# Block sums for a Winograd-Strassen down projection: made by DMAs that add in DRAM, with signs moved into the tokens' sums and three subtractions

## The chip, the cores and the metric

One core of a Trainium2 chip runs the kernel. The metric is the device time of one execution in microseconds: the median of three runs, and beside it the time of the one execution that the profiler recorded. TensorE (PE) multiplies; PEld is its loading of weights; VectorE (DVE), ScalarE (ACT) and GpSimd (POOL) work element by element; SyncE (SP) issues most of the DMAs. Each engine has its own stream of instructions and takes them in order: an instruction that waits holds back all that stand behind it on that engine, DMA issues too.

## What is computed

One block of an encoder on 512 tokens of width 1024, all in float32: three token mixers (an mLSTM, a neighbourhood attention, a cross-attention into a memory), merged by gates, then a gated feed-forward part and a last norm.

```python
def reference(x, mem, mix_norm_g, w_in, ...):
    for l in range(DEPTH):                      # DEPTH = 1
        h = rms_norm(x, mix_norm_g[l])
        proj = h @ w_in[l]
        ml_q, ml_k, ml_v, ml_o, ml_gates, na_qkv, xa_q, merge_pre = jnp.split(proj, split_points, axis=-1)
        ...
        merged = g_ml * (y_ml @ w_br_ml[l]) + g_na * (y_na @ w_br_na[l]) + g_xa * (y_xa @ w_br_xa[l])
        x = x + merged @ w_out[l]
        x = x + conv_glu_ffn(rms_norm(x, ffn_norm_g[l]), w_ffn_up[l], w_ffn_conv[l], b_ffn_conv[l], w_ffn_down[l])
    return rms_norm(x, final_norm_g)

def conv_glu_ffn(h, w_up, w_conv, b_conv, w_down):
    a, u = jnp.split(h @ w_up, 2, axis=-1)
    return (jax.nn.gelu(dwconv3(a, w_conv, b_conv)) * u) @ w_down
```

The change touches the last matrix product, `@ w_down`: 512 x 2816 times 2816 x 1024.

## The kernel before

**Precision.** A float32 product is made of three matmuls in a fast float32 format: every operand is split into a high part (ACT rounds a copy, `wh`) and a low part (DVE subtracts, `wl`), and `mm3` (L191) issues high x high, high x low and low x high.

**Weights.** All weights but those of the down projection lie in `wflat` in the order of their use, in blocks of 128 x 1024 (1088 in two of them): mlq, mlk, then eight token-major blocks ("tm"; two of 1088 columns, four and two of 1024), xaq, o, memk, memv, naq, nak, the gates and branches, out, and for the up projection pairs ua, uu. `weights(key)` (L180) hands out a block; before that it issues, by `emit_raw`, the loads up to three blocks ahead on SP's queue (tile `wr`, three buffers), and the splits up to one block ahead (`emit_split`). A load waits until the block three places before it has been split.

**Stages.** mlq and mlk (keys and queries), tm (values: `nv` tiles are written by ACT and DVE at L502 and L504 into scratch buffers and stored to `nav_d` by POOL at L506), the attention parts, the branches, the output projection, then 22 pairs of ua and uu (the loop at L1354), then the down projection.

**The down projection** is Strassen's scheme in Winograd's form on 2 x 2 blocks: the weights w_down are four blocks B11, B12, B22, B21 of 11 tiles of 128 x 512 each (`wdn` in DRAM), the hidden units four quarters `a11`, `a21`, `a12`, `a22`. Instead of eight block products it makes seven, p1 to p7, in the order of `ORDER`. Three of them need nothing but a block; the others need the sums T1 to T4 of blocks. Before the change these are made in SBUF, in the loop of the up projection, one of 11 tiles at a time: `sum_load` (L1250) has POOL load the tile of all four blocks; DVE makes T1 and T3 in one subtraction (L1272), T2 and T4 in one each (L1260, L1269); T3 and T2 are split (L1261 on ACT, L1264 on DVE); POOL stores high and low parts of T3 and T2 to `tsp` (L1266) and T1 and T4 unsplit to `tdn` (L1270). The loop takes three of these steps in a turn (L1389). In the down projection `raws_to` and `tiles_to` load them again.

**Order.** The program is written in the order of the text, but a scheduler places the instructions of each engine: an instruction that its own estimate calls ready may be placed ahead of others that stand before it in the text.

Of the kernel before, what the change touches and what calls it, by code (L numbers as in the profile page):

```python
# [11 lines left out]
F32 = mybir.dt.float32  # L12
# [5 lines left out]
P = 128  # L18
# [83 lines left out]
def hybrid_block(ctx, tc, xg, xT, memT, wflat, wdn, vecs, gbias, nabias, out):  # L102
# [18 lines left out]
    def unit(dt=F32):  # L121
        return up.tile([P, UNIT], dt, tag="unit", name=nm("u"))
# [11 lines left out]
        return atp.tile([P, 512], F32, tag="at", name=nm("at"))  # L134


    raws, split = {}, {}
    RAW_AHEAD, SPLIT_AHEAD = 3, 1
    st = {"raw": 0, "split": 0}
# [18 lines left out]
    def emit_split(i):  # L158
# [4 lines left out]
        for a, b in hs:  # L163
# [12 lines left out]
            for k in range(a, b):  # L176
                q = slice((k - a) * c, (k - a + 1) * c)
                split[i].append((h[:, q], l[:, q]))

    def weights(key):  # L180

        i, _, n = BINDEX[key]
        while st["raw"] <= min(i + RAW_AHEAD, len(BLOCKS) - 1):
            emit_raw(st["raw"])
            st["raw"] += 1
        while st["split"] <= min(i + SPLIT_AHEAD, len(BLOCKS) - 1):
            emit_split(st["split"])
            st["split"] += 1
        return split.pop(i)

    def mm3(ps, lh, ll, rh, rl, start, stop):  # L191
        PE.matmul(ps, lh, rh, start=start, stop=False)  # L192
# [885 lines left out]


    gens = []  # L1080

    quota = [0.0]

# [155 lines left out]
        A.activation(xt[t][:, hf * S:(hf + 1) * S], pt, AF.Copy)  # L1239


    HS = S // 2
    B11, B12, B22, B21 = range(4)
    T1, T4 = range(2)
    T3, T2 = range(2)
    tdn = dp.tile([2, P, HF * S], F32, name="tdn")
    tsp = dp.tile([2, 2, P, HF * S], F32R, name="tsp")
    sums = []

    def sum_load(k):  # L1250
        w = unit()[:, :4 * S]
        w4 = w.rearrange("p (q n) -> p q n", q=4)
        ks = slice(k * S, (k + 1) * S)
        G.dma_start(w4, wdn[:, :, ks].rearrange("q p n -> p q n"))
        q = [w[:, i * S:(i + 1) * S] for i in range(4)]
        hl = []

        def high():
            hl.append(unit(F32R)[:, :4 * S].rearrange("p (x q n) -> p x q n", x=2, q=2))
            V.tensor_tensor(q[B22], q[B22], q[B11], op=ALU.subtract)  # L1260
            A.activation(hl[0][:, 0], w4[:, 1:3], AF.Copy)  # L1261

        def low():
            V.tensor_tensor(hl[0][:, 1], w4[:, 1:3], hl[0][:, 0].bitcast(F32), op=ALU.subtract)  # L1264
            for x in range(2):
                G.dma_start(tsp[:, x, :, ks].rearrange("q p n -> p q n"), hl[0][:, x])  # L1266

        def store():
            V.tensor_tensor(q[B21], q[B21], q[B22], op=ALU.subtract)  # L1269
            G.dma_start(tdn[:, :, ks].rearrange("q p n -> p q n"), w4[:, 0:4:3])  # L1270

        sums.extend([lambda: V.tensor_tensor(w[:, :2 * S], w[:, S:3 * S], w[:, :2 * S], op=ALU.subtract), high, store, low])  # L1272


    PRODUCTS = {"p1": (wdn, B11), "p5": (tdn, T1), "p6": (tsp, T2), "p3": (wdn, B22), "p7": (tsp, T3), "p2": (wdn, B21),
                "p4": (tdn, T4)}
    GROUPS = ((0, 4), (4, 8), (8, HF))
# [51 lines left out]
    def early(g, i):  # L1329
        a11, a21, a12, a22 = quarters(g)  # L1330
        if i == 0:
            V.tensor_tensor(a21, a21, a22, op=ALU.add)
        else:
            V.tensor_tensor(a11, a21, a11, op=ALU.subtract)

    def ops_to(n):
        while ahead["op"] < min(n, len(OPS)):
            name, g = OPS[ahead["op"]]
            nk = GROUPS[g][1] - GROUPS[g][0]
            a11, a21, a12, a22 = quarters(g)  # L1340
            u = unit(F32R)
            h, l = u[:, :nk * HS], u[:, 1024:1024 + nk * HS]
            r3 = lambda t: t.rearrange("p (k s) -> p k s", s=HS)
            if name == "p3":
                V.tensor_tensor(a21, a22, a11, op=ALU.subtract)
                V.tensor_tensor(a11, a12, a11, op=ALU.subtract)
            src = {"p1": a11, "p5": a21, "p6": a11, "p3": a11, "p7": a21, "p2": a12, "p4": a22}[name]
            A.activation(r3(h), src, AF.Copy)  # L1348
            V.tensor_tensor(r3(l), src, r3(h).bitcast(F32), op=ALU.subtract)  # L1349
            ops[name, g] = h, l  # L1350
            ahead["op"] += 1

    SUMS = [2 + 4 * k // 3 for k in range(HF)]
    for f in range(FT):  # L1354
        i, j = divmod(f, HF)
        if j % 4 == 0:
            uu_[i][j // 4] = unit()
        ur = uu_[i][j // 4][:, j % 4 * S:(j % 4 + 1) * S]
        if f == 0:
            wa, wu = weights(("ua", f)), weights(("uu", f))  # L1360
            pa, pu = mmps(), mmps()
            x2sum = folded(acc2, S)
            for k in range(KT):
                if k < KT - 1:
# [46 lines left out]
    def add(name, c=None):  # L1411
        for t in range(2):
            if c is not None:
                V.tensor_tensor(cell(c, t), cell(c, t), Q[t], op=ALU.add)
                continue
            ps = banks[name][t]
            if name == "p1":
                Q.append(scr())
                A.activation(Q[t], ps, AF.Copy)
            if name in ("p6", "p7"):  # L1420
                V.tensor_tensor(Q[t], ps, Q[t], op=ALU.add)
            for c_ in {"p1": ((0, 0),), "p5": ((0, 1), (1, 1)), "p3": ((0, 1),), "p2": ((0, 0),)}.get(name, ()):
                V.tensor_tensor(cell(c_, t), ps, cell(c_, t), op=ALU.add)

# [203 lines left out]
```

## Time and profile before

| | us |
|---|---|
| median of three runs (861.78 to 862.62) | 862.36 |
| the profiled execution | 861.77 |
| its span, first to last instruction | 859.9 |
| VectorE busy in the span | 635.1 |
| ScalarE busy | 480.0 |
| GpSimd busy | 124.0 |
| DMA: 143.45 MB, mean | 167 GB/s |

Rows of groups read: line, engine, operation, output<-inputs by the program's names, shapes, count | busy time in us, mean of one in ns | idle time of the engine before them, and what ended it. Rows of a timeline: start in us from the span's start, duration in us, engine, line, operation. Rows of stretches ("560.00:690.00 ..."): length, then busy time and count of PE, PEld, DVE, ACT and POOL, the granted clock of TensorE, the DMA engines' busy share and GB/s. Rows of waits: who <- for whom: us in total, times, longest. Rows of DMA issues: output<-input, queue, count, KB each, median us from issue to landing. A row of a DMA queue: packets, MB, time as a share of 16 engines' span; q1 is SP's queue, q0 POOL's.

### The profile page before, as it was taken

Reading aid. Unit: us, or ns where it says so; the run is one execution under the profiler, and the core shown is the slowest. Engines: PE = TensorE matmul, PEld = TensorE weight load, DVE = VectorE, ACT = ScalarE, POOL = GpSimd, SP = SyncE. Lnnn points to the kernel's source line nnn. Section 1 sums busy time; section 2 is a strip of 40 time slices with the busy share of each in tenths; the row PEclk is TensorE's granted clock in tenths of the full one; section 3 lists DMA queues with packets and bytes.
Section 4 is the critical chain, followed back from the end, with each engine's and each line's share of the span. In section 5 each row is a group of like instructions: output and inputs, shape, how many; then the busy total and the mean of one; then the engine's idle time right before and its main releaser. Section 6 shows DMA issues by size and latency. Waiting matters only on the chain.

```text
span 859.9 us, 12078 instructions
## 1 busy us (share of the span) xinstructions
PE 852.0 (99%) x4152; PEld 719.2 (84%) x4152; DVE 635.1 (74%) x1317; ACT 480.0 (56%) x980; POOL 124.0 (14%) x234
## 2 busy tenths in 40 slices
PE   9999999999999999999999999999999999999996
PEld 7898889988888888888888888888888888888885
DVE  7774698997567758898667657777869777795694
ACT  7563467774445658888634446344444444553463
POOL 0101100000262460700000000121213010001101
PEclk9999999999999999999999999999999999999998
DMA  8233542442242354534325432595969572478942
GB/s 279 86 109 119 185 157 81 158 142 98 98 125 86 110 145 134 159 117 136 101 96 196 147 123 98 172 318 195 315 210 374 179 243 98 133 255 267 372 161 98
DMA packets 52477, 143.45 MB, mean 167 GB/s; under 512 B 6712, under 2 KB 11832, under 8 KB 52416
## 3 DMA queue, kind: packets, MB, share of 16 engines
q1 hardware_dynamic: 30800, 95.60, 32.8%
q0 software_dynamic: 21184, 46.69, 17.4%
q8 instruction: 33, 0.54, 0.3%
q10 hardware_dynamic: 432, 0.39, 0.1%
q14 instruction: 28, 0.23, 0.1%
HBM read 121.15 MB, written 21.51 MB: 166 GB/s over the span
## 4 chain that ended last, share of the span: by engine, by line
PE 99%; issue 0%; DVE 0%; POOL 0%; POOLq 0%; ACT 0%
PE mm L192 27%; PE mm L193 27%; PE mm L194 27%; PE at L193 4%; PE at L192 4%; PE at L194 4%; PE at L958 1%; PE at L939 1%; PE at L920 0%; PE at L921 0%; PE at L741 0%; PE at L789 0%; PE at L1238 0%; PE at L1046 0%; PE at L221 0%; PE mm L400 0%
## 5 line engine op out<-in xcount | busy, mean ns | idle before, releaser
L192 PE MATMUL mm<-u,wh 128*128 128x512 f32 (+1 forms) x907 | 353.3, 390 | 0.0
L194 PE MATMUL mm<-u,wl 128*128 128x512 f32 (+1 forms) x907 | 350.0, 386 | 0.0
L193 PE MATMUL mm<-u,wh 128*128 128x512 f32 (+1 forms) x907 | 349.7, 386 | 0.0
L174 ACT ACTIVATE wh<-wr 128x512 fp32r<-128x512 f32 (+1 forms) x256 | 160.2, 628 | 240.5 <-PE mm L193 195.8
L175 DVE TENSOR_TENSOR wl<-wr,wh 128x512 fp32r<-128x512 f32 (+2 forms) x258 | 174.9, 682 | 68.1 <-ACT wh L174 66.7
L194 PEld LDWEIGHTS mm<-u,wl 128*128 128x128 f32 x907 | 170.3, 188 | 34.6
L193 PEld LDWEIGHTS mm<-u,wh 128*128 128x128 f32 x907 | 170.6, 188 | 32.8
L192 PEld LDWEIGHTS mm<-u,wh 128*128 128x128 f32 x907 | 170.6, 188 | 32.7
L516 POOL DMA_DIRECT2D u<-nav_d x128 | 62.5, 545 | 69.8 <-DVE X L199 25.0
L193 PE MATMUL at<-wl,u 128*128 128x512 f32 (+2 forms) x130 | 43.9, 338 | 0.0
L194 PE MATMUL at<-wh,u 128*128 128x512 f32 (+2 forms) x130 | 43.8, 337 | 0.0
L192 PE MATMUL at<-wh,u 128*128 128x512 f32 (+2 forms) x130 | 43.7, 337 | 0.0
L1349 DVE TENSOR_TENSOR u<-u,u 128x1024 fp32r<-128x1024 f32 (+1 forms) x21 | 23.7, 1133 | 13.7 <-ACT u L1348 13.7
L1348 ACT ACTIVATE u<-u 128x1024 fp32r<-128x1024 f32 (+1 forms) x21 | 20.2, 980 | 20.1 <-PE mm L194 9.0
L193 PE MATMUL mm<-wl,u 128*128 128x512 f32 x80 | 31.3, 391 | 0.0
L194 PE MATMUL mm<-wh,u 128*128 128x512 f32 x80 | 31.2, 389 | 0.0
L192 PE MATMUL mm<-wh,u 128*128 128x512 f32 x80 | 31.0, 390 | 0.0
L438 ACT ACTIVATE s<-pad,vec 128x512 f32<-128x512 f32 x30 | 23.9, 813 | 9.0 <-DVE pad L436 9.0
L1266 POOL DMA_DIRECT2D tsp<-u x22 | 15.7, 716 | 77.6 <-ACT u L1261 72.0
L193 PEld LDWEIGHTS at<-wl,u 128*128 128x128 f32 x130 | 24.4, 188 | 2.8
L194 PEld LDWEIGHTS at<-wh,u 128*128 128x128 f32 x130 | 24.5, 188 | 2.5
L192 PEld LDWEIGHTS at<-wh,u 128*128 128x128 f32 x130 | 24.4, 188 | 2.7
(351 smaller groups left out, 1238.2 us busy)
## 6 DMA issues: line engine op xcount, KB each, us to landing
wr<-wflat SPq DMA_DIRECT2D x125, 512.0 KB, 3.4
u<-wdn POOLq DMA_DIRECT2D x11, 1024.0 KB, 8.0
tsp<-u POOLq DMA_DIRECT2D x22, 512.0 KB, 5.8
u<-tsp POOLq DMA_DIRECT2D x10, 1024.0 KB, 8.0
tdn<-u POOLq DMA_DIRECT2D x11, 512.0 KB, 3.7
nab<-nabias SPq DMA_DIRECT2D x16, 256.0 KB, 2.7
u<-nav_d POOLq DMA_DIRECT2D x128, 32.0 KB, 2.6
wr<-wdn SPq DMA_DIRECT2D x8, 512.0 KB, 4.5
```

The source lines that it names most:

```text
L174: A.activation(h[:, u:v], src, AF.Copy)
L175: V.tensor_tensor(l[:, u:v], src, h[:, u:v].bitcast(F32), op=ALU.subtract)
L192: PE.matmul(ps, lh, rh, start=start, stop=False)
L193: PE.matmul(ps, lh, rl, start=False, stop=False)
L194: st["mm"] = PE.matmul(ps, ll, rh, start=False, stop=stop).ins
L438: A.activation(t1, pad[:, 0:512], AF.Identity, scale=vcol(w, i), bias=vcol(b, i))
L516: G.dma_start(vw[r * 32:(r + 1) * 32, i * 256:(i + 1) * 256], nav_v[hf, r, CW[b]:CW[b] + 32, hp * 256:(hp + 1) * 256])
L939: PE.transpose(pt[:, j * P:(j + 1) * P], sm[:, j * P:(j + 1) * P], ident)
L958: PE.matmul(py[:, bl * 256:(bl + 1) * 256], vw[:, c:c + P], pp[bl][:, hf * 256:(hf + 1) * 256], start=hf == 0, stop=hf == 1)
L1266: G.dma_start(tsp[:, x, :, ks].rearrange("q p n -> p q n"), hl[0][:, x])
L1348: A.activation(r3(h), src, AF.Copy)
L1349: V.tensor_tensor(r3(l), src, r3(h).bitcast(F32), op=ALU.subtract)
```

## The change

The sums T1 to T4 are made in DRAM. `sum_ops` yields 24 DMA issues: for each of T1, T3, T2, T4 three copies on SP's queue (tiles 0-3, 4-7, 8-10 of the block) into `tdn`, and three transfers on POOL's queue that add a second block onto what was copied. As an adding transfer can only add, the sums have other signs: T1 = B11 + B12, T3 = B12 + B22, T2 = T1 + B22, T4 = T2 + B21; the tokens' sums and three steps of the last additions change theirs to match. `weights` issues one of the 24 at every second call from the first xaq block on. In the up projection remain the loads of T3 and T2 (now on SP's queue, two tiles at a time), their splits, and the stores of the parts to `tsp`.

```diff
+    tdn = dp.tile([4, P, HF * S], F32, name="tdn")
...
     def weights(key):
 
         i, _, n = BINDEX[key]
+        calls[0] += i >= BINDEX[("xaq", 0)][0]
+        if calls[0] % 2 and sums:
+            sums.pop(0)()
         while st["raw"] <= min(i + RAW_AHEAD, len(BLOCKS) - 1):
...
+    def sum_ops():
+        for dst, src, more in ((T1, wdn[B11], B12), (T3, wdn[B12], B22), (T2, tdn[T1], B22), (T4, tdn[T2], B21)):
+            for engine, s, kw in ((SY, src, {}), (G, wdn[more], dict(accum_op=ALU.add))):
+                for a, b in GROUPS:
+                    c = slice(a * S, b * S)
+                    yield lambda d=tdn[dst][:, c], s=s[:, c], e=engine, kw=kw: e.dma_start(d, s, **kw)
...
-    def sum_load(k):
-        w = unit()[:, :4 * S]
-        w4 = w.rearrange("p (q n) -> p q n", q=4)
-        ks = slice(k * S, (k + 1) * S)
-        G.dma_start(w4, wdn[:, :, ks].rearrange("q p n -> p q n"))
-        q = [w[:, i * S:(i + 1) * S] for i in range(4)]
+    parts = []
+
+    def sum_split(ks):
+        n = len(ks) * S
+        cs = slice(ks[0] * S, (ks[-1] + 1) * S)
+        v = lambda dt: unit(dt)[:, :2 * n].rearrange("p (q n) -> p q n", q=2)
+        w = v(F32)
+        SY.dma_start(w, tdn[T3:T2 + 1, :, cs].rearrange("q p n -> p q n"))
         hl = []
 
-        def high():
-            hl.append(unit(F32R)[:, :4 * S].rearrange("p (x q n) -> p x q n", x=2, q=2))
-            V.tensor_tensor(q[B22], q[B22], q[B11], op=ALU.subtract)
-            A.activation(hl[0][:, 0], w4[:, 1:3], AF.Copy)
-
-        def low():
-            V.tensor_tensor(hl[0][:, 1], w4[:, 1:3], hl[0][:, 0].bitcast(F32), op=ALU.subtract)
-            for x in range(2):
-                G.dma_start(tsp[:, x, :, ks].rearrange("q p n -> p q n"), hl[0][:, x])
-
-        def store():
-            V.tensor_tensor(q[B21], q[B21], q[B22], op=ALU.subtract)
-            G.dma_start(tdn[:, :, ks].rearrange("q p n -> p q n"), w4[:, 0:4:3])
-
-        sums.extend([lambda: V.tensor_tensor(w[:, :2 * S], w[:, S:3 * S], w[:, :2 * S], op=ALU.subtract), high, store, low])
+        def high(q):
+            if q == 0:
+                hl.extend([v(F32R), v(F32R)])
+            A.activation(hl[0][:, q], w[:, q], AF.Copy)
+
+        def low(q):
+            V.tensor_tensor(hl[1][:, q], w[:, q], hl[0][:, q].bitcast(F32), op=ALU.subtract)
+            if q == 1:
+                for x in range(2):
+                    G.dma_start(tsp[:, x, :, cs].rearrange("q p n -> p q n"), hl[x])
+
+        parts.extend([lambda: high(0), lambda: low(0), lambda: high(1), lambda: low(1)])
...
         if i == 0:
-            V.tensor_tensor(a21, a21, a22, op=ALU.add)
+            V.tensor_tensor(a21, a21, a22, op=ALU.subtract)
...
             if name == "p3":
-                V.tensor_tensor(a21, a22, a11, op=ALU.subtract)
-                V.tensor_tensor(a11, a12, a11, op=ALU.subtract)
+                V.tensor_tensor(a21, a22, a11, op=ALU.add)
+                V.tensor_tensor(a11, a12, a11, op=ALU.add)
...
-    SUMS = [2 + 4 * k // 3 for k in range(HF)]
+    SUMS = [2 + 5 * k // 2 for k in range((HF + 1) // 2)]
...
+        if f >= 3:
+            for _ in range(2):
+                if parts:
+                    parts.pop(0)()
         if f in SUMS:
-            sum_load(SUMS.index(f))
-        if f >= 4:
-            for _ in range(3):
-                if sums:
-                    sums.pop(0)()
+            k = 2 * SUMS.index(f)
+            sum_split(list(range(k, min(k + 2, HF))))
...
-                V.tensor_tensor(cell(c, t), cell(c, t), Q[t], op=ALU.add)
+                V.tensor_tensor(cell(c, t), cell(c, t), Q[t], op=ALU.subtract if c[1] else ALU.add)
...
-            if name in ("p6", "p7"):
+            if name == "p6":
                 V.tensor_tensor(Q[t], ps, Q[t], op=ALU.add)
+            if name == "p7":
+                V.tensor_tensor(Q[t], Q[t], ps, op=ALU.subtract)
```

Where the built programs place these instructions is told by their rows, engine by engine. A row has the line, the operation, output<-input with buffer numbers, the shape, and in brackets what it waits for: DMASWn are the eight counters that transfers from POOL use in turn, DMAHWn those of SP's, DVE and Activation the progress of these engines. The twelve adding transfers use DMASW0 to 7 and then 0 to 3: T1's groups 0, 1, 2, T3's 3, 4, 5, T2's 6, 7, 0 and T4's 1, 2, 3.

SP's queue before, from the third token-major block's load (`wr_534`) to the eighth's (`wr_782`):

```order
L150 DMA wr_534<-wflat 128x1024 [waits DMAHW6_49,DMAHW1_49,DVE_49]
L150 DMA wr_586<-wflat 128x1024 [waits DMAHW7_49,DMAHW2_49,DVE_49]
L150 DMA wr_644<-wflat 128x1024 [waits DMAHW0_49,DVE_49,Activation_49]
L150 DMA wr_714<-wflat 128x1024 [waits DMAHW4_49,DMAHW1_49,DVE_49]
L150 DMA wr_748<-wflat 128x1024 [waits DMAHW2_49,DVE_49]
L150 DMA wr_782<-wflat 128x1024 [waits DMAHW3_49,DVE_49]
```

The same place on SP's queue now: `wr_536` is the third token-major block's load, `wr_784` the eighth's, and `tdn<-tdn` are the copies of T2 (the first three) and T4 (the last three).

```order
L157 DMA wr_536<-wflat 128x1024 [waits DMAHW7_49,DVE_49]
L209 DMA tdn<-tdn 128x2048 [waits DMAHW0_49,DMASW0_49]
L157 DMA wr_588<-wflat 128x1024 [waits DMAHW2_49,DMAHW1_49,DVE_49]
L209 DMA tdn<-tdn 128x2048 [waits DMASW1_49]
L209 DMA tdn<-tdn 128x1536 [waits DMAHW3_49,DMASW2_49]
L209 DMA tdn<-tdn 128x2048 [waits DMAHW4_49,DMASW6_49]
L157 DMA wr_646<-wflat 128x1024 [waits DMAHW5_49,DVE_49,Activation_49]
L157 DMA wr_716<-wflat 128x1024 [waits DMAHW7_49,DMAHW6_49,DVE_49]
L209 DMA tdn<-tdn 128x2048 [waits DMASW7_49]
L157 DMA wr_750<-wflat 128x1024 [waits DMAHW1_49,DMAHW0_49,DVE_49]
L209 DMA tdn<-tdn 128x1536 [waits DMASW0_49]
L157 DMA wr_784<-wflat 128x1024 [waits DMAHW5_49,DMAHW2_49,DVE_49]
```

Six copies moved in among these loads; T4's three wait for T2's additions (DMASW6, 7, 0). The six copies of T1 and T3 stand ahead of these rows, the first of them behind the load that left at 18.61 us before.

POOL before, from its last small fills to the first stores of nv:

```order
L576 MEMSET num 128x32 [waits Pool_49]
L476 MEMSET u_579 128x16
L506 DMA nav_d<-nv_851 128x512 [waits DVE_49,Activation_49]
L506 DMA nav_d<-nv_857 128x512 [waits DVE_49,Activation_49]
L506 DMA nav_d<-nv_863 128x512 [waits DVE_49,Activation_49]
```

The same place on POOL now, from T2's last two additions on:

```order
L209 DMA tdn<-wdn 128x2048 [waits DMAHW2_49]
L209 DMA tdn<-wdn 128x1536 [waits DMAHW3_49,DMASW0_49]
L209 DMA tdn<-wdn 128x2048 [waits DMAHW4_49,DMASW1_49]
L209 DMA tdn<-wdn 128x2048 [waits DMAHW7_49,DMASW2_49]
L209 DMA tdn<-wdn 128x1536 [waits DMAHW1_49,DMASW3_49]
L526 DMA nav_d<-nv_853 128x512 [waits DMASW4_49,DVE_49,Activation_49]
L526 DMA nav_d<-nv_859 128x512 [waits DMASW5_49,DVE_49,Activation_49]
```

All twelve additions moved in ahead of the eight nav_d stores; each waits on POOL for its copy (DMAHWn), and the last of the stores for T4's last addition (DMASW3, not among these rows).

More of the change, by code (lines that the diff above doesn't have):

```diff
@@ L134, in atps @@
         return atp.tile([P, 512], F32, tag="at", name=nm("at"))
+    HS = S // 2
+    B11, B12, B22, B21 = range(4)
+    T1, T4, T3, T2 = range(4)
+    GROUPS = ((0, 4), (4, 8), (8, HF))
+    tdn = dp.tile([4, P, HF * S], F32, name="tdn")
+    tsp = dp.tile([2, 2, P, HF * S], F32R, name="tsp")
     raws, split = {}, {}
@@ L178, in emit_split @@
                 split[i].append((h[:, q], l[:, q]))
+    sums = []
+    calls = [0]
     def weights(key):
         i, _, n = BINDEX[key]
+        calls[0] += i >= BINDEX[("xaq", 0)][0]
+        if calls[0] % 2 and sums:
+            sums.pop(0)()
         while st["raw"] <= min(i + RAW_AHEAD, len(BLOCKS) - 1):
@@ L1080, in hybrid_block @@
     gens = []
+    sums.extend(sum_ops())
     quota = [0.0]
@@ L1239, in turn @@
         A.activation(xt[t][:, hf * S:(hf + 1) * S], pt, AF.Copy)
[L1242 to L1248, printed above, removed]
-    def sum_load(k):
-        w = unit()[:, :4 * S]
-        w4 = w.rearrange("p (q n) -> p q n", q=4)
-        ks = slice(k * S, (k + 1) * S)
-        G.dma_start(w4, wdn[:, :, ks].rearrange("q p n -> p q n"))
-        q = [w[:, i * S:(i + 1) * S] for i in range(4)]
-        hl = []
-        def high():
-            hl.append(unit(F32R)[:, :4 * S].rearrange("p (x q n) -> p x q n", x=2, q=2))
-            V.tensor_tensor(q[B22], q[B22], q[B11], op=ALU.subtract)
-            A.activation(hl[0][:, 0], w4[:, 1:3], AF.Copy)
-        def low():
-            V.tensor_tensor(hl[0][:, 1], w4[:, 1:3], hl[0][:, 0].bitcast(F32), op=ALU.subtract)
-            for x in range(2):
-                G.dma_start(tsp[:, x, :, ks].rearrange("q p n -> p q n"), hl[0][:, x])
-        def store():
-            V.tensor_tensor(q[B21], q[B21], q[B22], op=ALU.subtract)
-            G.dma_start(tdn[:, :, ks].rearrange("q p n -> p q n"), w4[:, 0:4:3])
-        sums.extend([lambda: V.tensor_tensor(w[:, :2 * S], w[:, S:3 * S], w[:, :2 * S], op=ALU.subtract), high, store, low])
@@ L1275, in hybrid_block @@
-    PRODUCTS = {"p1": (wdn, B11), "p5": (tdn, T1), "p6": (tsp, T2), "p3": (wdn, B22), "p7": (tsp, T3), "p2": (wdn, B21),
+    parts = []
[5 more added lines that the diff above has]
+        SY.dma_start(w, tdn[T3:T2 + 1, :, cs].rearrange("q p n -> p q n"))
+        hl = []
+        def high(q):
[8 more added lines that the diff above has]
+        parts.extend([lambda: high(0), lambda: low(0), lambda: high(1), lambda: low(1)])
@@ L1276, in hybrid_block @@
+    PRODUCTS = {"p1": (wdn, B11), "p5": (tdn, T1), "p6": (tsp, T2 - T3), "p3": (wdn, B22), "p7": (tsp, 0), "p2": (wdn, B21),
                 "p4": (tdn, T4)}
-    GROUPS = ((0, 4), (4, 8), (8, HF))
     TILES = [(n, k) for n in ORDER for k in range(HF)]
```

## The prediction

> **What bounds the kernel now.** I read the page first: busy times, then the chain of work that ended last.
>
> ```profile
> PE 852.0 (99%) x4152; PEld 719.2 (84%) x4152; DVE 635.1 (74%) x1317; ACT 480.0 (56%) x980; POOL 124.0 (14%) x234
> ...
> PE 99%; issue 0%; DVE 0%; POOL 0%; POOLq 0%; ACT 0%
> ```
>
> The matmuls fill 99% of the span and 99% of the chain. A busy share can hide pauses, since ends of matmuls are modelled, so next I asked for the waits of the weight loads into the array (PEld), over the whole run:
>
> ```profile
> PEld L221 <- issue: 0.7, 1, 0.7
> PEld mm L409 <- ACT u L342: 0.3, 1, 0.3
> PEld mm L193 <- DVE wl L1319: 0.3, 1, 0.3
> ```
>
> Three waits, 1.3 us in all, none of them where the change works. TensorE takes one matmul behind the other from start to end. So no engine that is relieved can give more than about a microsecond, and the question is only whether the change makes TensorE wait.
>
> **What is removed, and why it gives nothing.** Most of what goes was in the up projection:
>
> ```profile
> L1272 DVE TENSOR_TENSOR u<-u 128x1024 f32<-128x1024 f32 x11 | 13.4, 1218 | 1.4 <-DMA u<-wdn 1.4
> L1260 DVE TENSOR_TENSOR u<-u 128x512 f32<-128x512 f32 x11 | 7.5, 684 | 0.0
> L1269 DVE TENSOR_TENSOR u<-u 128x512 f32<-128x512 f32 x10 | 6.9, 687 | 0.1
> 560.00:690.00 130.00, 130.00 (x585) 107.60 (x584) 101.30 (x141) 58.04 (x86) 26.29 (x36) 1.00 0.78 265
> ```
>
> The three VectorE operations leave, 11 times (1218 + 684 + 687) ns = 28.5 us (one of the last kind lies outside the rows' window). In 560 to 690 us, where most of them stand, VectorE was busy 101.3 of 130 us and TensorE all 130. The idle time of an engine for which nobody waits grows: 0 us. The splits into high and low parts stay, two blocks at a time. The other signs in the tokens' sums (additions for subtractions and the reverse) keep shapes and engines: 0 us. The new loads of T3 and T2 stand in SP's queue with the weights there; the stores they replace leave POOL's, and the DMA share of 0.78 has room: 0 us.
>
> **What is added, and where.** 11 tiles of 128 x 512 float32 are 2.884 MB for each of four sums: 11.5 MB of copies on SP's queue, and 11.5 MB of adding transfers on POOL's. In the code they are spread from the first xaq block on; the order of the built program puts them earlier, into the mlk and token-major (tm) stages, and there they stand between things for which others wait.
>
> On SP the copy of T4's first group waits for the addition of T2's first group, its second and third copies for T2's second and third additions. Behind these three stand the weight loads of tm blocks 5, 7 and 8 (of eight) and all later ones. The last of them, the load of tm block 8, left SP at 67.73 us:
>
> ```profile
> 18.61 0.33 SPq L150 DMA_DIRECT2D wr<-wflat  x1
> 67.73 0.33 SPq L150 DMA_DIRECT2D wr<-wflat  x1
> 81.73 0.39 PE L192 MATMUL mm<-wh,u 128*128 128x512 f32 x1
> 82.41 0.28 PE L192 MATMUL at<-wh,u 128*128 128x256 f32 x1
> 93.72 0.39 PE L192 MATMUL mm<-u,wh 128*128 128x512 f32 x1
> wr<-wflat SPq DMA_DIRECT2D x125, 512.0 KB, 3.4
> L174 ACT ACTIVATE wh<-wr 128x512 fp32r<-128x512 f32 (+1 forms) x256 | 160.2, 628 | 240.5 <-PE mm L193 195.8
> L175 DVE TENSOR_TENSOR wl<-wr,wh 128x512 fp32r<-128x512 f32 (+2 forms) x258 | 174.9, 682 | 68.1 <-ACT wh L174 66.7
> ```
>
> The second PE row is the first matmul of block 7, the third that of the first xaq block: blocks 7 and 8 run from 82.41 to 93.72, so block 8 starts at 88.06. (Three matmuls of 512 columns take 82.41 - 81.73 = 0.68 us, a block of 24 of them 5.45.) It needs 3.4 us of landing and 0.63 + 0.68 us for its first half's split before: its load may leave as late as 83.35 us, a slack of 15.6 us. The first copy leaves behind the load of 18.61, at 19 us.
>
> **How long the transfers take.** Prices come from the queues' rows, and that transfers of both queues share the engines from the landing times in a crowded stretch (first row below, 560 to 620 us) beside a quiet one (480 to 540 us):
>
> ```profile
> q1 hardware_dynamic: 30800, 95.60, 32.8%
> q0 software_dynamic: 21184, 46.69, 17.4%
> ...
> wr<-wflat SPq DMA_DIRECT2D x11, 512.0 KB, 5.5
> ...
> wr<-wflat SPq DMA_DIRECT2D x11, 512.0 KB, 3.3
> ```
>
> q1 needed 32.8% of 859.9 us for 95.60 MB, 2.95 us per MB with all 16 engines; q0 3.20. The same weight load landed in 5.5 instead of 3.3 us beside POOL's transfers. A copy inside DRAM and an addition stand in no row. Copy: cheap end, one load (2.95: each byte is read and written once, as in any load); dear end, a load plus a store, 5.9. I take 2.95, the nearest row. Addition: cheap end, one POOL transfer, 3.2; dear end, three passes (read, read, write), 9.6. I take 6.4, since two things are read, which no row here does at once.
>
> T2's last addition can land when the engines have done what was queued with or ahead of it since 19 us:
> - copies of T1, T3, T2 and two groups of T4: 8.65 + 2.10 = 10.75 MB x 2.95 = 31.7 us
> - additions of T1, T3, T2: 8.65 MB x 6.4 = 55.4 us
> - eight weight loads, 4.26 MB x 2.95 = 12.6 us
>
> Together 99.7 us, so 118.7 us; with about 1 us of landing and 0.3 us for the copy's issue, block 8's load leaves at 120.0 instead of 83.35 at the latest: 36.7 us late. That load now lands behind T4's last copy (0.79 MB, 2.3 us), shared packet by packet with T4's additions: another 6 us, so 42.7.
>
> A pause also slows what follows it. The first matmuls of the program:
>
> ```profile
> 0.78 3.15 PE L221 MATMUL at<-const-bfloat16-1.0 128*128 128x256 bf16 x14 [0.78 <-PEq L1621]
> 3.76 0.58 PE L409 MATMUL mm<-u,wh 128*128 128x256 f32 x1
> ...
> 85.24 0.28 PE L192 MATMUL at<-wh,u 128*128 128x256 f32 x1
> 85.35 0.28 PE L193 MATMUL at<-wl,u 128*128 128x256 f32 x1
> 85.47 0.28 PE L194 MATMUL at<-wh,u 128*128 128x256 f32 x1
> ...
> 853.00:860.00 7.00, 0.00 (x0) 0.00 (x0) 1.89 (x4) 1.94 (x4) 0.54 (x1) 0.68 0.39 150
> ```
>
> 14 of 256 columns took 2.98 us, 0.213 each, against 0.118 later; after TensorE's end the granted clock falls to 0.68. A restart from a cold array costs 1.3 us; the late loads come one by one, so I count four: 5.2 us. **Sum: 42.7 + 5.2 = 47.9 us.**
>
> POOL has a chain of its own. The adding transfers wait on POOL for their copies, and all twelve stand ahead of the eight nav_d stores:
>
> ```profile
> 80.59 0.73 POOL L506 DMA_DIRECT2D nav_d<-nv  x1 [42.56 <-DVE nv L504]
> 93.92 0.47 ACT L502 ACTIVATE nv<-at,rc_x 128x256 fp32r<-128x256 f32 x1
> 106.12 1.22 DVE L563 TENSOR_TENSOR_SCAN s<-s,at 4x512 f32<-4x512 f32 x1
> nav_d<-nv POOLq DMA_DIRECT2D x8, 256.0 KB, 2.5
> ```
>
> T4's additions end at 118.7 + 2.3 (last copy) + 18.5 (2.884 MB x 6.4) + 4.6 (three loads) = 144 us. The first nav_d store passes behind them, 146 us, instead of at 83. ACT's last nv, at 93.92 before, needs that buffer: 52 us late, and behind it stands the split for the second xaq block, which starts at 93.72 + 5.45 = 99.2: 148 us, 48.6 late. This is as late as the SP chain already makes it, so it adds nothing to the sum; but curing one of the two queues alone would save little.
>
> The profiled execution took 861.8 us, 1.9 over its span and 0.6 under the median of 862.36. 861.8 + 47.9 = 909.7, **910 us**.
>
> **What the Trainium skill says of these prices.** In DMA: Bandwidth & Descriptors, section Latency and other measured facts, copies between tensors in HBM ran at 207 to 214 GB/s per direction, about 4.8 us per MB; by that the copies of the sum would cost 51.6 instead of 31.7 us and the time would be 930. No run shown here has such a copy; the rival on copies below is this rule at a dearer price. In Collectives: The Full Stack, section The bandwidth ceiling, reducing runs at half of a copy's rate, because the addition needs two source reads on one ring; by it an addition costs two copies, which with that page's copy price would add another 28 us. Nothing in this trace adds in a DMA.
>
> **Rivals.**
> 1. Copies pay both sides (5.9 us per MB). For it: source and target are the same memory. Against it: nothing measured. 31.7 us more: 942.
> 2. Additions cost no more than a plain transfer (3.2). The work is 72.0 us, so T2's last addition lands at 92, the load leaves 9.0 us late, plus 4 for its landing and two restarts, 2.6: 877.
> 3. Not slower: the transfers stay inside the slack. This needs block 8's load on its way by 83.35 us, 63 us after the first copy's issue and landing. Copies and loads take 44.3 of them; 18.7 us are left for 8.65 MB of additions, so it decides at 2.2 us per MB, less than a plain transfer's 3.2. For it: the rows below, in which the DMA engines (last share, 0.26 to 0.39) are idle two thirds of 48 to 84 us, and the rows cannot show whether both queues' transfers inside DRAM share the engines as loads do. Against it: 5.5 us for 3.3 above. Time 862.
> ```profile
> 48.00:60.00 12.00, 12.00 (x96) 11.88 (x95) 9.09 (x17) 7.01 (x12) 0.00 (x0) 1.00 0.35 124
> 60.00:72.00 12.00, 12.00 (x58) 10.00 (x57) 6.25 (x26) 5.39 (x10) 0.00 (x0) 1.00 0.26 91
> 72.00:84.00 12.00, 12.00 (x61) 10.21 (x60) 5.47 (x13) 6.08 (x13) 1.81 (x3) 1.00 0.39 131
> ```
>
> 4. Additions far dearer, 19.2 us per MB (each packet waits for its own reads): 166 us of additions, 111 us more than in the sum: about 1020.
> 5. Relief of VectorE counts after all: at most the 0.3 us of L1319 and a few tenths, 861 to 862. This is not faster by what a measurement can tell (about 0.2%, 1.7 us).
>
> **Numbers.** Forecast's prices, 890 to 925: 0.40. Rival 1, 925 to 974: 0.25. Rival 2, 866 to 890: 0.15. Rival 3: 0.08. Rival 4 and all else above 974: 0.10. Faster by over 0.2%: 0.02. Both dear ends together (5.9 and 9.6: 159 us of work, 96 us late, 10 for the landing, 5 for restarts) give 973, both cheap ends 877, a little less where the engines overlap better; the range 866 to 974 leaves out 2 in 10. Slower 0.90, same 0.08, faster 0.02.
>
> **What would show it.** Right: SP's wait rows name the additions (tdn) before weight loads, from about 55 us on; TensorE idle between 70 and 150 us, with a granted clock below 1 there; POOL's nav_d stores near 130 to 146 us; everything after 200 us the old trace shifted by one constant; VectorE some 28 us less busy with no time gained there. Landing times of the adding transfers and copies give the two prices. Wrong: T2's last addition lands before 83 us, or SP shows no wait for it; or the new time stands in the up projection, where SP's loads of the sums wait for free buffers ahead of weight loads; I cost that at 0 because the weight loads have as much slack there (blocks of 5.45 us, three ahead), and were it gone, a late load would cost its lateness above 15 us.

## The result and the profile after

The changed kernel takes 898.23 us (median of 4 runs, 897.01 to 900.08) against 862.49 of the kernel before on the same chip (861.78 to 862.71): a ratio of 1.0418, with a 95% interval of 1.0397 to 1.0438, or 35.7 us more. The profiled execution has a span of 895.8 us, 35.9 above that of before. On the page (busy times, then the clock and the DMA engines in 40 slices of 22.4 us, then the chain that ended last):

```profile
PE 862.9 (96%) x4152; PEld 724.5 (81%) x4152; DVE 609.7 (68%) x1285; ACT 477.8 (53%) x981; POOL 110.4 (12%) x214
...
PEclk9988699999999999999999999999999999999999
DMA  8999995254325245463422343476567342478952
...
PE 90%; DMA 7%; DVE 1%; ACT 1%; issue 1%; SPq 0%; POOL 0%; POOLq 0%; ACTq 0%; DVEq 0%
```

Two things are read from the first row. TensorE issued the same 4152 matmuls, but was busy 862.9 instead of 852.0 us: its matmuls ran slower by 10.9 us in all. The rest of the 35.9, 25.0 us, is idle time. The second and third rows say where: in slices 2 to 6 (22 to 134 us) the DMA engines are full, and in 3 to 5 the clock granted to TensorE is down. The chain, 99% PE before, now holds 7% of DMA.

The stretches (length; busy time and count of PE, PEld, DVE, ACT, POOL; clock; DMA share; GB/s) put bounds on it. The share adds up the times of packets, so full engines can read a little over 1:

```profile
20.00:40.00 20.00, 20.00 (x90) 16.57 (x89) 15.11 (x31) 11.51 (x18) 3.31 (x4) 1.00 0.94 284
40.00:60.00 20.00, 15.09 (x88) 13.18 (x86) 11.12 (x18) 9.28 (x16) 3.75 (x9) 0.97 1.03 315
60.00:80.00 20.00, 16.10 (x73) 14.13 (x74) 6.39 (x14) 5.28 (x11) 1.75 (x3) 0.76 1.02 278
80.00:100.00 20.00, 6.63 (x23) 4.93 (x22) 2.95 (x17) 1.74 (x3) 2.44 (x3) 0.67 1.02 252
100.00:120.00 20.00, 18.41 (x90) 15.54 (x91) 7.93 (x20) 7.68 (x16) 3.85 (x6) 0.83 1.03 304
...
200.00:560.00 360.00, 360.00 (x1768) 304.30 (x1767) 260.62 (x644) 221.87 (x526) 68.54 (x136) 1.00 0.40 119
560.00:690.00 130.00, 130.00 (x590) 107.59 (x589) 82.59 (x119) 60.35 (x90) 7.22 (x10) 1.00 0.63 215
```

Nearly all of the loss lies between 40 and 120 us. In 560 to 690 us, where VectorE is now busy 82.59 us instead of 101.3, TensorE is busy 130 of 130 as before: the relief (25.4 us over the whole span) brought nothing. TensorE's rows (start, duration, line, operation; in brackets the idle time ahead and who ended it) name three pauses:

```profile
54.87 0.39 PE L212 MATMUL at<-wh,u 128*128 128x272 f32 x1 [0.17 <-ACT wh L181]
60.22 0.60 PE L213 MATMUL at<-wl,u 128*128 128x272 f32 x1 [4.96 <-DVE wl L182]
...
78.90 0.50 PE L212 MATMUL mm<-wh,u 128*128 128x512 f32 x1 [2.12 <-ACT wh L181]
...
101.59 0.79 PE L212 MATMUL mm<-wh,u 128*128 128x512 f32 x1 [14.96 <-ACT wh L181]
102.31 0.79 PE L213 MATMUL mm<-wl,u 128*128 128x512 f32 x1
```

They stand in tm blocks 2, 4 and 5; each time the split (ACT, DVE) waited for its weight block, as ACT's waits in 40 to 103 us show:

```profile
ACT wh L181 <- DMA wr<-wflat: 42.5, 6, 19.1
```

In matmuls compared one by one with the run before (the order is the same), the delay is 10.5 us after tm block 2, 14.9 after block 4, 30 at the first matmul of block 5, 32.7 from the end of block 5 to the first xaq blocks, and 35.5 at the end: from the start of block 5 on it is nearly all slow matmuls that add. The 512-column matmuls behind the long pause last 0.79 us instead of 0.39.

SP's queue shows both kinds of delay. First its longest wait for additions, then its rows around the copies of T4 (the three tdn<-tdn behind 47.20 are T2's last two and T4's first), then the landing times of what left SP in 28 to 50 us, after and before:

```profile
SPq L209 <- DMA tdn<-wdn: 48.9, 5, 33.8
```

```profile
46.81 0.33 SPq L157 DMA_DIRECT2D wr<-wflat  x1
47.20 41.20 SPq L209 DMA_DIRECT2D tdn<-tdn  x3
88.49 1.00 SPq L157 DMA_DIRECT2D wr<-wflat  x2
...
100.72 0.47 SPq L209 DMA_DIRECT2D tdn<-tdn  x1
102.89 19.84 SPq L157 DMA_DIRECT2D wr<-wflat  x5
```

```profile
wr<-wflat SPq DMA_DIRECT2D x2, 544.0 KB, 17.2
...
wr<-wflat SPq DMA_DIRECT2D x2, 512.0 KB, 29.2
```

```profile
wr<-wflat SPq DMA_DIRECT2D x2, 544.0 KB, 3.4
wr<-wflat SPq DMA_DIRECT2D x2, 512.0 KB, 3.4
```

T4's first copy held SP's queue until 87.9 us, and block 5's load left at 88.49. But the four loads ahead of it, which left SP on time, landed 15 to 31 us after their issue (the rows have the median of each two) where 3.4 was usual. So there were two explanations:

- **Wait theory** (the prediction's words): SP stands at T4's copies until T2's additions have landed, and the weight loads behind them leave late.
- **Throughput theory**: 23 MB of transfers fill the DMA engines; a load behind large copies in SP's queue lands late whenever it leaves, and the wait only takes the place of a wait in the queue.

### The profile page after: what moved, and what is told of

It reads as the page before. It is cut to its first block, busy times and chain, and to the rows that moved or that the text cites. A ratio compares the mean times of both kernels' runs of the same rounds, so it can differ in the third digit from the quotient of the medians.

```text
span 895.8 us, 12018 instructions
## 1 busy us (share of the span) xinstructions
PE 862.9 (96%) x4152; PEld 724.5 (81%) x4152; DVE 609.7 (68%) x1285; ACT 477.8 (53%) x981; POOL 110.4 (12%) x214
## 3 DMA queue, kind: packets, MB, share of 16 engines
HBM read 138.45 MB, written 38.81 MB: 198 GB/s over the span
## 4 chain that ended last, share of the span: by engine, by line
PE 90%; DMA 7%; DVE 1%; ACT 1%; issue 1%; SPq 0%; POOL 0%; POOLq 0%; ACTq 0%; DVEq 0%
PE mm L212 25%; PE mm L213 24%; PE mm L214 24%; DMA tdn<-tdn 4%; PE at L213 4%; PE at L214 4%; PE at L212 4%; DMA wr<-wflat 2%; DMA tdn<-wdn 1%; PE at L978 1%; PE at L959 1%; PE at L940 0%; PE at L941 0%; PE at L761 0%; PE at L809 0%
## 5 line engine op out<-in xcount | busy, mean ns | idle before, releaser
L213 PE MATMUL at<-wl,u 128*128 128x512 f32 (+2 forms) x130 | 45.9, 353 | 6.3 <-DVE wl L182 6.3
L212 PE MATMUL mm<-wh,u 128*128 128x512 f32 x80 | 32.7, 411 | 17.1 <-ACT wh L181 17.1
L1282 POOL DMA_DIRECT2D tsp<-u x12 | 8.7, 721 | 313.6 <-ACT u L1276 305.5
L212 PE MATMUL at<-wh,u 128*128 128x512 f32 (+2 forms) x130 | 45.2, 349 | 0.2 <-ACT wh L181 0.2
L214 PE MATMUL at<-wh,u 128*128 128x512 f32 (+2 forms) x130 | 45.2, 348 | 0.0
L213 PE MATMUL mm<-wl,u 128*128 128x512 f32 x80 | 33.4, 418 | 0.2 <-DVE wl L182 0.2
L456 DVE TENSOR_TENSOR pad<-mm,rb 128x512 f32<-128x512 f32 x22 | 15.2, 693 | 27.1 <-PE mm L214 27.1
L212 PEld LDWEIGHTS mm<-wh,u 128*128 128x128 f32 x80 | 15.8, 198 | 21.3 <-ACT wh L181 17.9
L214 PE MATMUL mm<-wh,u 128*128 128x512 f32 x80 | 32.4, 405 | 0.0
L459 DVE SCALAR_TENSOR_TENSOR s<-pad,vec,s 128x512 f32<-128x512 f32 x30 | 22.2, 750 | 13.5 <-ACT s L458 13.4
```

The lines of the kernel that those rows point to most:

```text
L213: PE.matmul(ps, lh, rl, start=False, stop=False)
L214: st["mm"] = PE.matmul(ps, ll, rh, start=False, stop=stop).ins
L456: V.tensor_tensor(pad[:, 1:513], ps, rbt, op=ALU.mult)
L459: V.scalar_tensor_tensor(t1, pad[:, 1:513], vcol(w, n + i), t1, op0=ALU.mult, op1=ALU.add)
```

## The experiments

All times are medians beside runs of the kernel before on the same chip (861.9 to 862.5 us); ratios are to it.

| run | early in the mlk/tm stages | us | ratio (95%) |
|---|---|---|---|
| the change | 12 copies on SP, 12 additions on POOL | 898.23 | 1.0397 to 1.0438 |
| e2 | the same, no copy waits for an addition | 898.25 | 1.0402 to 1.0433 |
| e3 | T1, T3, T2 | 886.58 | 1.0253 to 1.0305 |
| e6 | T1, T3 | 872.05 | 1.0098 to 1.0129 |
| e7 | copies alone | 862.50 | 0.9998 to 1.0016 |
| e12 | additions made plain copies | 880.62 | 1.0196 to 1.0230 |
| e1 | none; spread from the first xaq block's place (85 us) on | 885.55 | 1.0250 to 1.0285 |
| e5 | none; spread from the first naq block's place (171 us) on | 863.11 | 0.9999 to 1.0017 |
| e4 | all on POOL's queue, from 2.6 us on | 905.47 | 1.0489 to 1.0535 |
| e9 | all on POOL's queue, from 19 us on | 896.76 | 1.0387 to 1.0418 |
| e10 | the change, nav_d's stores on ACT's queue | 896.85 | 1.0389 to 1.0424 |
| e11 | e9 and e10 together | 888.15 | 1.0287 to 1.0317 |
| e8 | (before, without its subtractions) | 862.54 | 0.9995 to 1.0013 |

**e2: the wait taken away, the bytes left.**

```diff
-        for dst, src, more in ((T1, wdn[B11], B12), (T3, wdn[B12], B22), (T2, tdn[T1], B22), (T4, tdn[T2], B21)):
+        for dst, src, more in ((T1, wdn[B11], B12), (T3, wdn[B12], B22), (T2, wdn[B11], B22), (T4, wdn[B21], B21)):
```

> T2 and T4 are copied from input blocks (B11 and B21) and not from T1 and T2, so that no copy waits for an addition; their sums then lack the terms that T1 and T2 would have brought. Bytes, queues and order stay. Throughput theory: unchanged, 895 to 901, since the loads still stand behind the same work. Wait theory: the pause of 15 us at the fifth token-major block goes, and with it its cold restart of 2.5: 877 to 883. The rest, some 15 us from the loads that land late behind copies, stays under both.

Measured: 898.25, unchanged. The row of SP's queue and the landing times of what left it in 61.5 to 76 us show what took the wait's place:

```profile
62.01 10.58 SPq L157 DMA_DIRECT2D wr<-wflat  x2
```

```profile
wr<-wflat SPq DMA_DIRECT2D x2, 512.0 KB, 34.4
```

Block 5's load now leaves SP at 62.01, 26.5 us earlier than in the change, and TensorE still starts block 5 at 99.4 instead of 101.6: its load lands 36.6 us after its issue (the row has the median of two). The wait theory falls: a wait in one place was exchanged for another in the same queue.

**e3 and e6: fewer bytes.** T4's copies (e3), or T2's and T4's (e6), are held behind a weight load of their place in the text.

```diff
+    def sum_issue(d, s, e, kw, dst):
+        with tc.issue_after(st["sp"]) if e is SY and dst == T4 else nullcontext():
+            e.dma_start(d, s, **kw)
```

(`st["sp"]` is the last weight load; e6 has `dst in (T2, T4)`.)

> Only T4's three copies (and so its additions) are held to their place in the text, past the token-major blocks; T1, T3 and T2 stay early. SP then has no wait on an addition of T2 among the token-major loads, and 5.8 MB of the 23 leave the crowded stretch. Wait theory: the pause at the fifth block goes, some 15 us left: 877 to 881. Throughput theory: the other 17.3 MB still fill the engines ahead of the loads, so about 25 us remain: 885 to 890.

> T2's and T4's copies are both held to their place past the token-major blocks, T1 and T3 stay early: 11.5 of the 23 MB remain in the crowded stretch. Throughput theory, as a queue worked through with measured prices (2.6 us per MB copied or loaded, 5.0 added): only the second token-major block's load is late, by 11 us, the later ones land in time: 871 to 876. A theory in which the loss goes with the megabytes (35.7 us for 23 MB): 880. A theory in which only waits on additions count: 862.

Measured: 24.4 and 10.0 us above before, both inside what throughput said, and neither in proportion to the bytes: 11.5, 17.3 and 23.1 MB cost 10.0, 24.4 and 35.7 us. In e6 only one place waits, tm block 2, where it loses 9.6 us (compared matmul by matmul) and the change lost 10.5:

```profile
PE at L217 <- DVE wl L182: 6.4, 2, 4.3
PE at L245 <- PEq L1639: 0.8, 1, 0.8
PE mm L217 <- DVE wl L182: 0.2, 1, 0.2
```

**e7: the copies alone**, at the same places of SP's queue (`(G, wdn[more], ...)` left out of `sum_ops`).

> The 12 additions are left out, so every sum lacks its second term; the 12 copies stay where the change has them, ahead of the same weight loads in SP's queue. Throughput theory: 11.5 MB at 2.6 us per MB are 30 us of the engines, spread over 40 us with loads between: 862 to 866. The theory that the place in SP's queue is what costs (a load behind two or three copies lands 8 to 10 us late whatever POOL does): 870 to 877.

Measured: 862.50, no loss. The landing times of what left SP in 30 to 80 us in this run, that stretch, then the same stretch in the change:

```profile
wr<-wflat SPq DMA_DIRECT2D x8, 512.0 KB, 4.4
```

```profile
30.00:80.00 50.00, 50.00 (x265) 43.44 (x264) 34.73 (x79) 28.41 (x46) 2.67 (x8) 1.00 0.79 288
```

```profile
30.00:80.00 50.00, 41.19 (x205) 35.60 (x204) 26.40 (x51) 21.42 (x35) 7.74 (x14) 0.89 1.03 291
```

The loads stand behind the same copies, but the engines are busy 0.79 of the time, the loads land in 4.4 us and not in 29, and TensorE is busy 50 of 50 us. Both moved the same GB/s: it is not the rate of moved bytes that shows that engines are full, but their busy share. A place in the queue alone costs nothing.

**e12: additions made plain copies**, to test the price of adding.

```diff
-            for engine, s, kw in ((SY, src, {}), (G, wdn[more], dict(accum_op=ALU.add))):
+            for engine, s, kw in ((SY, src, {}), (G, wdn[more], {})):
```

> The changed kernel with the twelve adding transfers made plain copies of the same bytes, on the same queue, in the same places of both queues, with the same waits: the sums then hold the second term alone. If an addition's price lies in its second read, a packet of 8 KB falls from 628 to about 310 ns, T2's additions land at about 80 and not 101: worked through as a queue 871 (at 2.6 us per MB) to 876 (at 3.2); the prediction's rival with cheap additions gave 877. If the price belongs to POOL's queue or to two queues sharing the engines, and not to the adding: 895 or more.

Measured: 880.62, outside of both stated ranges and between them. Rows of POOL's queue for 19 to 150 us, by when its additions and the nav_d stores are done (packets, MB, share of 131 us of 16 engines), in e12, in the change, and in e7, where the queue has the nav_d stores alone:

```profile
q0 software_dynamic: 2944, 13.65, 29.5%
```

```profile
q0 software_dynamic: 2944, 13.65, 49.2%
```

```profile
q0 software_dynamic: 1216, 2.11, 5.2%
```

Without the stores (2.11 MB, 6.8 us), the change's additions took 64.5 - 6.8 = 57.7 us for 11.54 MB, 5.0 us per MB; the plain copies 38.6 - 6.8 = 31.8 us, 2.76. In single packets of 8 KB the median is 628 ns for an addition and 309 for a copy, the latter on either queue. So the price lies in the adding, and it is about that of two copies. That the second half is a second read, as the prediction argued, no row shows: the profile counts 138.45 MB read from HBM in both runs. The time fell by 17.6 us, less than the 22 to 27 that the queue worked through gave: the kernel stays 18.7 us above before, as the copies of both queues still fill the engines (the share ahead of the GB/s):

```profile
40.00:60.00 20.00, 17.87 (x110) 16.09 (x110) 14.87 (x23) 10.12 (x16) 2.71 (x8) 1.00 1.01 355
60.00:80.00 20.00, 14.93 (x76) 11.92 (x74) 5.90 (x24) 6.54 (x12) 1.69 (x4) 0.95 0.96 332
80.00:100.00 20.00, 12.74 (x46) 10.06 (x47) 5.62 (x14) 5.92 (x12) 2.16 (x5) 0.71 1.01 378
```

**e1 and e5: where the text puts them.** All copies are held behind the weight load of their place in the text (the edit of e3 without `dst == T4`); in e5 the 24 issues also begin at a later block:

```diff
-        calls[0] += i >= BINDEX[("xaq", 0)][0]
+        calls[0] += i >= BINDEX[("naq", 0)][0]
```

> All 24 transfers are kept, but the copies are held behind the weight load that stands ahead of them in the text, so that they run from the first xaq block on, a few per weight block. Throughput theory (TensorE waits because 23 MB of transfers fill the DMA engines for 80 us just where eight weight loads must land) and wait theory (it waits because T4's copies hold SP's queue until T2's additions have landed) both expect 862 us, plus or minus 2, with no wait of TensorE. The rival that the transfers cost something wherever they stand expects 872 or more. If VectorE's 25 us less of busy time are worth anything, this is the run that would show it: below 860.

> As the run with all copies held to their place, but the first of the 24 is issued at the first naq block and not at the first xaq block: no transfer of the sums then runs before about 175 us, past the gates' chain of the mLSTM (rd stored, R and memT loaded, lfc), where that run lost 16 to 17 of its 23 us; the rest it lost up to 208 us. If transfers cost only where a load that TensorE needs at once must land: 862 to 866, with no wait of TensorE longer than 2 us. The rival that this much traffic costs wherever it stands, some 1 us per MB: 880 or more. If 25 us less of VectorE were worth anything: below 860.

e1 was a miss: 885.55, not 862. Its pause is elsewhere, ahead of the mLSTM's gates: TensorE waits for `lfc`, a tile of the gates that ACT writes, and on ACT that instruction stands behind those that read the loads of `memT`, the transposed memory. First TensorE's waits, then ACT's rows:

```profile
PE at L628 <- ACT lfc L619: 15.3, 1, 15.3
PE at L804 <- DVE H L796: 3.2, 1, 3.2
```

```profile
122.26 0.63 ACT L487 ACTIVATE s<-s 128x512 f32<-128x512 f32 x1 [7.52 <-DMA s<-memT]
...
131.97 0.63 ACT L487 ACTIVATE s<-s 128x512 f32<-128x512 f32 x1 [7.77 <-DMA s<-memT]
...
133.31 0.48 ACT L619 ACTIVATE lfc<-at 128x400 f32<-128x400 f32 x1
```

T1's three copies and three additions were issued from 85 to 122 us. The loads of memT landed late (10.0 us at the median from 100 us on, against 3.7 before). The last of them also left late: on SP it now stands behind a load of R, which waited for the store of rd:

```profile
SPq L670 <- DMA rd<-s: 10.2, 1, 10.2
```

So here too a late small transfer and a place in a queue act together; the runs do not part the two for e1. All of its loss lies before 208 us, though T2's and T4's 12 transfers came after that. e5, whose first copy stands behind these loads, takes 863.11, at most 0.17% more than before by its interval, and the largest group of waits ahead of TensorE is 0.8 us:

```profile
PEld mm L217 <- DVE wl L1334: 0.8, 2, 0.4
```

So the transfers cost where a load that is needed at once must land beside them, and at most 0.17% here, where none is. It also means that the change, put well, is no faster than before.

**e4, e9, e10, e11: one queue cured at a time.** The prediction held that SP's queue and POOL's (nav_d's stores behind the additions) delay about equally, so that curing one saves little. In e4 POOL issues the copies too:

```diff
-            for engine, s, kw in ((SY, src, {}), (G, wdn[more], dict(accum_op=ALU.add))):
+            for engine, s, kw in ((G, src, {}), (G, wdn[more], dict(accum_op=ALU.add))):
```

> The copies are issued on POOL's queue with the additions; SP's queue has the weight loads alone, as before the change. The prediction said that curing one of the two queues alone saves little, because nav_d's stores stand behind all twelve additions on POOL: by it 890 or more, with the pause now at the xaq blocks (ACT's nv waits for a buffer, the split behind it). The rival that POOL's chain is harmless and SP's queue is all expects 862 to 870.

Measured: 905.47. The run has a fault as a test: POOL has nothing to do at the start, so the copies began at 2.56 us and not at 19, among the first loads of tokens. 24 of its 43 us were lost before 44 us, as the stretch of 5 to 30 us shows (TensorE busy 12 of 25):

```profile
5.00:30.00 25.00, 12.00 (x41) 8.17 (x40) 4.59 (x9) 4.68 (x8) 4.10 (x6) 0.82 1.03 296
```

e9 repeats it with a first copy that waits on POOL for a value written at about 18 us. e10 is the change with the nav_d stores issued on ACT's queue, and e11 has both:

```diff
+            if k == 4:
+                st["go"] = G.tensor_copy(tiny(1), sq[:, :1]).ins
...
+        with tc.issue_after(st["go"]):
+            e.dma_start(d, s, **kw)
```

```diff
-                G.dma_start(nav_d[t * P:(t + 1) * P, (c - 1) * 512:c * 512], nv)
+                A.dma_start(nav_d[t * P:(t + 1) * P, (c - 1) * 512:c * 512].bitcast(F32), nv.bitcast(F32))
```

> As the run with the copies on POOL's queue, but the first copy waits (by a copy of one column on POOL, added for this) until about 18 us, when the change issues it, so that the stage of the tokens' loads is as before. SP's queue has weight loads alone: cured. POOL's has the copies and additions ahead of nav_d's stores, as the prediction feared. Worked through with the measured prices: the weight loads share the engines packet by packet and land in 8 us, inside the slack; T2's additions end at 100 to 105, the first nav_d store lands some 12 later, ACT's nv at 93.92 waits for it: 880 to 890. The prediction (curing one queue alone saves little): 885 or more. Rival that POOL's chain is harmless: 862 to 868.

> The changed kernel with the eight nav_d stores issued on ACT's queue, so that they no longer stand behind the additions on POOL; the copies stay on SP. The prediction put POOL's chain at nothing beside SP's: 895 to 901. Rival that the nav_d stores carry part of the loss: 892 or less.

> Both cured, at the same place and with the same bytes: copies and additions on POOL's queue from about 18 us on, weight loads alone on SP's, nav_d's stores on ACT's. If what costs is that loads queue behind large transfers (each load then waits for at most one large packet per packet of its own): 862 to 868. If full engines cost wherever loads queue: 880 or more.

Measured: 896.76 and 896.85 with one queue cured, 1.5 and 1.4 us below the change, which is inside the intervals of the ratios. In e9 the delay is 0 up to the end of the tm blocks and then comes at the xaq blocks, where ACT waits for nav_d's stores:

```profile
ACT nv L528 <- DMA nav_d<-nv: 22.0, 1, 22.0
```

My estimate for e9, 880 to 890, was too low; the prediction's "885 or more" held. In e11 both are cured, and it is neither 862 to 868 nor a loss in the same place. Its stretches, the landing times of the weight loads issued in 19 to 127 us, then ACT's row:

```profile
30.00:100.00 70.00, 69.73 (x397) 61.54 (x396) 42.56 (x99) 35.70 (x61) 13.07 (x23) 1.00 1.03 299
100.00:140.00 40.00, 22.91 (x89) 16.72 (x87) 15.78 (x26) 10.40 (x22) 5.09 (x8) 0.79 0.94 271
```

```profile
wr<-wflat SPq DMA_DIRECT2D x13, 512.0 KB, 11.4
```

```profile
126.84 0.63 ACT L489 ACTIVATE s<-s 128x512 f32<-128x512 f32 x1 [15.85 <-DMA s<-memT]
```

For 70 us the engines are as full as in the change (1.03), and TensorE is busy 69.73 of 70 us: weight loads that have a queue of their own land in 11.4 us, inside their slack. Then memT's load comes late, as in e1, the split that TensorE needs stands behind its use on ACT, and nearly all of the 26 us are lost there and just behind. Together with e7: neither full engines nor a place behind copies makes TensorE wait for the tm blocks' loads, only both at once; and a kernel that escapes that meets the next load with less slack, until the transfers are over.

**e8: the relief alone.** The kernel before without the three groups of subtractions that make the sums in the up projection (`V.tensor_tensor(..., op=ALU.subtract)` in `sum_load`; the one in `low`, which makes the low parts, stays).

> The kernel before, without the 33 VectorE subtractions that make the sums in the up projection (the sums are not made, their loads, splits and stores stay). The prediction put this relief at nothing: 862, within 1.5 of the kernel before. The rival that VectorE's 28 us matter: 859 or less.

Measured: 862.54 against 862.07, a ratio of 0.9995 to 1.0013.

## Why the prediction was right, and what was mis-sized

**What bounds the kernel** was read rightly: TensorE waits for nobody, so relieving VectorE is worth nothing (e8, and e5 where the change's traffic does no harm), and the question was only whether the change makes TensorE wait.

**Place and sign** were right: transfers moved ahead of the tm blocks' loads, the pause with a lowered clock in the tm stage, nothing after 200 us but a shift that is constant to 0.7 us, SP's wait for additions. The pauses began at 55 us, not 70, the nav_d stores left from 114 to 130 us, not near 130 to 146, and VectorE was relieved of 25.4 us, not 28.

**The sum** was 47.9 us, measured 35.7. Three of its terms were mis-sized, two too large and one too small:

- *Copies at 2.95 and additions at 6.4 us per MB.* The measured prices are 2.62 (SP's queue in 19 to 127 us, row below: 45.2% of 108 us for 18.66 MB, copies and loads together) and 5.0 (e12). With them the work to T2's last addition is 10.75 x 2.62 + 8.65 x 5.0 + 4.26 x 2.62 = 82.6 us, not 99.7, so it lands at 102 instead of 119. T4's third copy, which waits for it, left at 100.72, and block 8's load at 102.89 instead of 120.0.

```profile
q1 hardware_dynamic: 3658, 18.66, 45.2%
```

- *36.7 us late at block 8 and 6 for its landing.* Block 8's load left 19.5 us after its latest time of 83.35. But block 8 was not what decided: from the end of block 5 on the delay stays at 32.7 us, so nobody waited for block 8's load. Block 5 already started 30 us late, and 15 us of that came earlier, from loads that left SP on time and landed 15 to 31 us later. The prediction gave a landing behind copies 6 us once, at the last block; it had to be asked for every load behind a copy.
- *Restarts, 4 x 1.3 us.* TensorE's busy time rose by 10.9 us, not 5.2. (The rows beside the term give 0.115 us for a later matmul and not 0.118, so 1.4 us a restart; and rival 1's sum is 941, not 942. Neither changes the forecast.)

Idle 25.0 and slow matmuls 10.9 give the span's 35.9. That 910 came within 12 us of 898 is in part luck: the sum was worked out for a load that did not decide, and its dear prices stood in for late landings and slow matmuls that it did not count.

**The step that named the cause** was right in its reckoning and wrong in its words. It said that T4's copies wait on SP for T2's additions and that the loads behind them leave late. e2 took this wait away and nothing changed. What the sum in fact counted, the engines' work ahead of the load, is what the runs bear out: price (e12), bytes (e3, e6) and a shared queue (e7, e11).

**POOL's chain**, "adds nothing" and "curing one of the two queues alone would save little", held: 1.5 and 1.4 us of 35.7 (e9, e10), no more than the noise. Curing both would still have left 26 (e11).

**The rivals.** Copies that pay for both sides (5.9 per MB) fell: a copy inside DRAM costs per byte what a load costs (309 ns per packet of 8 KB, a weight load's packets of 4 KB 160). The Trainium skill, DMA: Bandwidth & Descriptors, section Latency and other measured facts, has 207 to 214 GB/s per direction for copies between tensors in HBM, an estimate of 4.8 us per MB; those were copies of 16 KB per partition, rows far apart. Here, with 6 or 8 KB per partition, the trace differs: 309 ns per 8 KB packet on each of 16 engines, 424 GB/s or 2.4 us per MB. Cheap additions fell too, as e12 shows beside the change. Collectives: The Full Stack, section The bandwidth ceiling, of the same skill says that reducing runs at half of a copy's rate because of its two source reads; here the trace agrees on the half, 628 against 309 ns, and does not show the second read. The rival "not slower" decided at 2.2 us per MB of additions; they cost 5.0.

## What to carry to other kernels

Where a change adds DMA traffic, work out the engines' time ahead of each load that has little slack, with the additions at the price of two copies (5.0 against 2.76 us per MB here), and ask this of every such load, not of the last one alone: taking a wait away, or moving one queue, only hands the delay to the next load while the engines are full. The same traffic was all but free where no load was needed at once (e5), so its place in the program is worth more than its queue. And before moving work off an engine, see whether the bounding engine waits for it at all.

## What the runs showed of the hardware that was not expected

- A slower clock after pauses costs much: 25.0 us of idle time, nearly all in three pauses, brought 10.9 us of slower matmuls, with a granted clock of 0.67 in 80 to 100 us and 0.83 in the 20 us behind, and 512-column matmuls of up to 0.79 us instead of 0.39.
- A queue of its own does not keep small stores quick beside full engines: nav_d's stores of 256 KB, with 2.7 us to landing in e7, took 22.8 us at the median on ACT's queue in e11 in 40 to 100 us, longer than the weight loads' 11.6 there. Whether their packets of 2 KB or their standing behind one another is the reason, the runs do not show.
- The moved GB/s does not tell full engines from others: 288 in e7 at a share of 0.79, 291 in the change at 1.03.
